# DeltaNet on one core: 64-row inverses applied twice with A's block between, side work after every third matmul, another order of the last two head blocks

## The chip, the cores and the metric

The kernel runs on one core of a Trainium2 chip. The metric is the device time of one execution in microseconds; lower is better. The core has a matrix engine (TensorE, PE in the rows, with its weight loads as PEld), a vector engine (VectorE, DVE), ScalarE (ACT), GpSimd (POOL) and DMA queues, of which SyncE (SP) and POOL issue most here.

## The reference

One layer of a streaming encoder over 16 meta rows plus 1024 prompt rows, and over 64 rows of a running stream. `xn = RMSNorm(h)` goes through one input projection of 2048 x 8208; 1024 channels feed a gated short convolution (mixer A) and 8 heads of 128 a gated DeltaNet (mixer B); an output projection of 2048 x 2048, a residual and a last RMSNorm follow. Mixer B works in chunks of 64 rows (cut, and written shorter):

```python
    kk = jnp.einsum('nbhid,nbhjd->nbhij', kc * bc[..., None], kc) * decay
    a_mat = jnp.where(strict, kk, 0.0) + eye
    t_mat = lax.linalg.triangular_solve(a_mat, eye, left_side=True, lower=True, unit_diagonal=True)
    u = t_mat @ (vc * bc[..., None])
    w = t_mat @ (kc * (bc * jnp.exp(gc))[..., None])
    qk = jnp.einsum('nbhid,nbhjd->nbhij', qc, kc) * decay

    def step(s, inp):
        v_new = u_i - w_i @ s
        o = (q_i * jnp.exp(g_i)[..., None]) @ s + qk_i @ v_new
        s = s * jnp.exp(g_last) + (k_i * jnp.exp(g_last - g_i)[..., None]).T @ v_new
        return s, o
```

The result of a chunk's `step` depends on the state `s` of the chunk before it; `t_mat` does not.

## The kernel before

The 1104 rows are the free dimension, in three pieces of 336, 384 and 384 columns. All weights and activations of the projections are split into a high and a low part, so that a product of two float32 numbers is three fast matmuls (high by high, low by high, high by low). A **job** is one tile of 128 output channels: 16 slices `k` of the contraction, three pieces, three matmuls, so 144 main matmuls into the PSUM tiles `pj`. There are 64 tiles: mixer A's block j has four jobs (AC, AX, AZ, AB), a head of mixer B has four (K, Q, V, Z). The string `order` sets in which order these blocks of four jobs run. After each job its PSUM tiles are read by VectorE, convolved and gated (the list `convs`), and written to DRAM scratch.

The DeltaNet of a head works in three steps p of three chunks of 128 rows each, 24 steps in all. Each is a **front** (`dn_front`) and later a **back** (`dn_back`). The front transposes q and k for their norms (PE `psq`, `psk`), builds the decays, multiplies k with k and q (PE `psm`), and gives three matrices A of 128 rows (`bm`) over DRAM to GpSimd, which inverts their 32-row diagonal blocks by elimination: DMA `e_in<-bm` on SP, then on POOL the DMA `eT<-e_in`, 60 small operations (`tm`, `eT`), the DMA `e_out<-eT` and the DMA `t<-e_out` back into the tile `t32` (`t` in the rows). The back waits for that tile. It adds the identity and transposes it in 32-row blocks on DVE (`t<-t,cst`, `ti<-t`), joins the blocks of 32 to 64 rows (`psx`, `psy` of 128 columns), then those of 64 to 128 rows (a second `psy`, `psx`, `psy`, each three matmuls of 64 x 64), and transposes v (`psv`). Then follow three chunks, one after the other: `psr` (k by the state) and r on DVE, `psu` (the inverse by r) and u on ACT, `psn` with the new state sn, and two matmuls into `po` for the output. After the third chunk the outputs are normalised on DVE (`on`) and transposed (`pot`).

PE takes its instructions in one order, with fronts and backs as **side work** between the main matmuls. A planner in the kernel sets that order while the program is written. It keeps estimated clocks `clk` of PE, DVE and ACT (`mm`, `tr` and the class `Timed` advance them). Front and back are generators: after `yield d` the next step is due at the largest of the three clocks plus d. `pump()` is called between main matmuls and writes out each step that is due by the PE clock; it also writes steps of `convs` while DVE's clock is less than 0.7 us ahead of PE's. A back starts when `el_done`, the planner's due time of the elimination, has passed: GpSimd is taken to be busy for `EL[1]` us from `EL[0]` us after the front's last step, or from the end of the elimination before. At most one finished front waits for its back, besides the one being written. On DVE the program order is kept; on PE and ACT the framework's scheduler may move instructions a little against the order in which they were written.

After the next-to-last job the fronts and backs left over are run to their end; then come the last job and the output projection, with `po` matmuls of 512 columns.

All vector operations are recorded at L61 (the helper), matmuls at L83, transposes on PE at L87.

Of the kernel before, what the change touches and what calls it, by code (L numbers as in the profile page):

```python
# [17 lines left out]
P = 128  # L18
# [48 lines left out]
def hymba_kernel(ctx: ExitStack, tc: tile.TileContext, hT, x_prompt, x_sample, w_in, w_ba, w_out, cst1, cst2, par,  # L67
# [348 lines left out]
    NFIRST = len(jobs)  # L416
    order = "b0 b1 b2 b3 a2 b4 a3 b5 a4 b6 a5 b7 a6 a7"
    for o in order.split():
# [8 lines left out]
    def project(js, first=lambda k: None, pool=pj):  # L427
# [5 lines left out]
        for kc in range(0, NK, 4):  # L433
            for kind, i, w, pieces in js:
                wh, wl = stream[0].get()
                first(kc)
                for k in range(kc, kc + 4):
                    for p in pieces:
                        a, n = 0 if p else SKIP[kind, w], PIECES[p][1]
                        o = ps[kind, i, w, p][:, a:n]  # L440
                        mm(o, wh[:, k - kc, :], xh[p][:, k, a:n], k == 0, False)
                        mm(o, wh[:, k - kc, :], xl[p][:, k, a:n], False, False)
                        mm(o, wl[:, k - kc, :], xh[p][:, k, a:n], False, k == NK - 1)
                    pump()
        flush_convs()
# [317 lines left out]
    def psd(name):  # L763
        return pd.tile([P, 4, P], F32, tag="pd", name=name)

    EL = (5.0, 50.0)
    t32 = [dn.tile([P, 3, P], F32, tag=f"t32_{i}", name=f"t32_{i}") for i in range(2)]
    for i in range(2):
        V.memset(t32[i], 0.0)
        Q.dma_start(whole(e_out[i]), t32[i])  # L770

    def dn_front(h, p):
# [58 lines left out]
        for c in range(3):  # L831
            pm = psd("psm")
            mm(pm[:, 0:2, :], kq[:, c, 0, :], kq[:, c, :, :], True, True)
            V.scalar_tensor_tensor(bm[:, c, :], pm[:, 0, :], cq[:, 9 + c:10 + c], bm[:, c, :], ALU.mult, ALU.mult)
            V.tensor_tensor(at[:, c, :], pm[:, 1, :], at[:, c, :], ALU.mult)
            yield 0.0
# [21 lines left out]
    def dn_back(h, p):  # L858
# [7 lines left out]
        V.transpose(ti.rearrange("p c t -> p (c t)"), tn.rearrange("p c t -> p (c t)"))  # L866
        b32 = tmp("b32", "b32", 1)
        V.tensor_tensor(b32, bm, cst[:, None, C_M32:C_M32 + P].to_broadcast([P, 3, P]), ALU.mult)
        yield 0.3
        px = psd("psx")  # L870
# [3 lines left out]
        S.copy(x, px[:, 0:3, :])  # L874
        yield 0.3
        py = psd("psy")
# [3 lines left out]
        V.tensor_tensor(tt, ti, py[:, 0:3, :], ALU.add)  # L880
        py2 = psd("psy2")
        for c in range(3):
            mm(py2[:64, c, 0:64], x[0:64, c, 0:64], tn[0:64, c, 0:64], True, True)
        t64 = b32[0:64, :, 64:128]
        V.tensor_tensor(t64, tn[0:64, :, 0:64], py2[0:64, 0:3, 0:64], ALU.add)
        yield 0.3
        px2 = psd("psx2")
        for c in range(3):
            mm(px2[0:64, c, 0:64], bm[64:128, c, 0:64], tt[64:128, c, 64:128], True, True)
        y64 = b32[0:64, :, 0:64]  # L890
        S.copy(y64, px2[0:64, 0:3, 0:64])
        yield 0.3
        py3 = psd("psy3")
        for c in range(3):
            mm(py3[0:64, c, 0:64], t64[:, c, :], y64[:, c, :], True, True)
        S.copy(tt[0:64, :, 64:128], py3[0:64, 0:3, 0:64])

# [12 lines left out]
        else:  # L910
            yield 0.3
        po = po_.tile([P, 4, P], F32, tag="po", name="po")
        for c in range(3):
# [8 lines left out]
            else:  # L922
                mm(pr[:, 0, :], kq[:, c, 0, :], s, True, True)
                V.scalar_tensor_tensor(r, pr[:, 0, :], cq[:, 6 + c:7 + c], vb[:, c, :], ALU.mult, ALU.add)
            yield 0.25
            pu = psd("psu")
# [19 lines left out]
            state[h] = sn  # L946
            yield 0.2
        if p == 2:
# [306 lines left out]
```

## Time and profile before

| | |
|---|---|
| three runs | 2256.23 us median, 2255.58 to 2258.77 |
| the profiled execution | 2254.53 us, of which its span from the first to the last instruction 2252.7 us |
| PE busy | 2200.5 us (98%) |
| DVE busy | 1346.3 us (60%) |
| POOL busy | 877.6 us (39%) |
| ACT busy | 603.0 us (27%) |
| mean granted TensorE clock | 0.997 |

A float32 matmul of the side work is one instruction in the program and two records in the trace, a main matmul is one in both. A matmul's end in the trace is modelled and lies beyond the start of the next, so the price of a matmul is read from starts, not from its duration.

### The profile page before, as it was taken

The numbers are of one execution on the slowest core, as the hardware profiler recorded it, in microseconds if no ns is written. First come the engines' busy times: TensorE is split into PE (matmuls) and PEld (weight loads), VectorE is DVE, ScalarE is ACT, GpSimd is POOL, SyncE is SP. The second block draws the span as 40 slices with busy tenths as digits, with TensorE's granted clock in tenths as the row PEclk, the third lists the DMA queues.
The fourth block names the chain that finished last, engine by engine and source line by source line (L and its number), as shares of the span: only waits on it lengthen the run. The fifth ranks groups of instructions, "written<-read, shape, count | busy, mean of one in ns | idle before, by whom it ended". The sixth has DMA issues, their size and how long they took to land.

```text
span 2252.7 us, 35780 instructions
## 1 busy us (share of the span) xinstructions
PE 2200.5 (98%) x12938; PEld 2065.4 (92%) x12938; DVE 1346.3 (60%) x3538; ACT 603.0 (27%) x1482; POOL 877.6 (39%) x1517
## 2 busy tenths in 40 slices
PE   8999999999999999999999999999999999999997
PEld 8999899999999999999999999999999987788886
DVE  6653475777675557565765576557664445474544
ACT  7232121222222122221222222122222125444341
POOL 0000038374666656455565666655564400000000
PEclk9999999999999999999999999999999999999999
DMA  7223132232222222322222222222322138664652
GB/s 261 77 88 94 39 92 80 81 94 81 90 74 88 66 64 85 89 67 78 91 87 64 75 79 89 63 73 78 94 70 75 50 126 270 208 198 147 224 169 84
DMA packets 162068, 231.13 MB, mean 103 GB/s; under 512 B 17756, under 2 KB 89636, under 8 KB 161764
## 3 DMA queue, kind: packets, MB, share of 16 engines
q1 hardware_dynamic: 156356, 217.30, 30.8%
q0 software_dynamic: 3072, 7.11, 1.6%
q10 hardware_dynamic: 2464, 4.46, 0.5%
q8 instruction: 101, 1.65, 0.3%
q14 instruction: 75, 0.61, 0.1%
HBM read 184.61 MB, written 44.17 MB: 102 GB/s over the span
## 4 chain that ended last, share of the span: by engine, by line
PE 87%; DVE 9%; DMA 2%; ACT 1%; issue 1%; SPq 0%; DVEq 0%; ACTq 0%
PE pj L83 61%; PE po L83 17%; DVE acc L61 3%; PE psy L83 2%; PE psx L83 1%; DMA yr<-yscr 1%; PE psm L83 1%; DVE wl L61 1%; PE psn L83 1%; PE pjb L83 1%; PE psu L83 1%; PE psr L83 1%; ACT jk L61 1%; DVE rot L61 1%; PE psv L87 1%
## 5 line engine op out<-in xcount | busy, mean ns | idle before, releaser
L83 PE MATMUL pj<-xh,wh 128*128 128x384 f32 x2048 | 692.9, 339 | 11.7 <-DVE raw L61 4.2
L83 PE MATMUL pj<-xl,wh 128*128 128x384 f32 x2048 | 690.6, 337 | 1.0 <-DVE xl L61 1.0
L83 PE MATMUL pj<-xh,wl 128*128 128x384 f32 x2048 | 688.5, 337 | 0.0
L61 DVE TENSOR_TENSOR wl<-wr,wh 128x512 fp32r<-128x512 f32 x464 | 337.3, 729 | 334.5 <-ACT wh L61 329.7
L83 PE MATMUL pj<-x,wh 128*128 128x320 f32 (+3 forms) x2048 | 522.3, 335 | 7.0 <-ACT x L61 7.0
L61 ACT CAST wh<-wr 128x512 fp32r<-128x512 f32 x464 | 285.9, 618 | 864.0 <-PE pj L83 666.6
L847 POOL TENSOR_TENSOR tm<-eT 12x30 f32<-12x30 f32 (+4 forms) x720 | 399.8, 555 | 122.9 <-DMA eT<-e_in 68.3
L849 POOL TENSOR_TENSOR eT<-eT,tm 12x30 f32<-12x30 f32 (+4 forms) x720 | 422.9, 587 | 56.4
L83 PEld LDWEIGHTS pj<-xh,wh 128*128 128x128 f32 x2048 | 385.3, 188 | 17.8 <-issue 5.8
L83 PEld LDWEIGHTS pj<-xl,wh 128*128 128x128 f32 x2048 | 385.0, 188 | 2.5 <-DVE xl L61 1.7
L83 PEld LDWEIGHTS pj<-xh,wl 128*128 128x128 f32 x2048 | 384.8, 188 | 0.0
L83 PEld LDWEIGHTS pj<-x,wh 128*128 128x128 f32 x2048 | 350.0, 191 | 16.5 <-ACT x L61 7.3
L83 PE MATMUL pj<-x,wl 128*128 128x320 f32 (+3 forms) x1024 | 320.8, 313 | 6.2 <-DVE wl L61 6.2
L842 POOL DMA_DIRECT2D eT<-e_in x24 | 17.4, 723 | 639.6 <-DMA e_in<-bm 326.6
L83 PE MATMUL po<-wh,yh 128*128 128x512 f32 x656 | 238.8, 396 | 3.1 <-DVE yh L61 2.8
L83 PE MATMUL po<-wl,yh 128*128 128x512 f32 x528 | 209.0, 397 | 1.9 <-DVE wl L61 1.9
L83 PEld LDWEIGHTS pj<-x,wl 128*128 128x128 f32 x1024 | 194.3, 190 | 7.8 <-DVE wl L61 7.8
L1113 POOL TENSOR_TENSOR hres<-hres,fw 128x512 f32<-128x512 f32 x1 | 1.7, 1732 | 469.4 <-ACT hres L61 469.4
L83 PEld LDWEIGHTS po<-wh,yh 128*128 128x128 f32 x656 | 123.1, 188 | 34.8 <-DVE yh L61 4.0
L61 DVE SCALAR_TENSOR_TENSOR acc<-raw,pk,acc 128x384 f32<-128x384 f32 (+1 forms) x216 | 147.3, 682 | 6.1
L83 PE MATMUL po<-wh,yl 128*128 128x512 f32 x336 | 132.8, 395 | 0.0
L83 PEld LDWEIGHTS po<-wl,yh 128*128 128x128 f32 x528 | 99.1, 188 | 27.1 <-DVE wl L61 3.4
(243 smaller groups left out, 2140.2 us busy)
## 6 DMA issues: line engine op xcount, KB each, us to landing
wr<-in_w_in SPq DMA_DIRECT2D x288, 256.0 KB, 3.1
wr<-in_w_out SPq DMA_DIRECT2D x176, 256.0 KB, 2.8
scr<-acc SPq DMA_DIRECT2D x48, 192.0 KB, 2.3
kq<-scr SPq DMA_DIRECT2D x48, 192.0 KB, 3.2
hres<-in_x_prompt SPq DMA_DIRECT2D x32, 256.0 KB, 5.2
yr<-yscr SPq DMA_DIRECT2D x32, 192.0 KB, 3.3
scr<-co SPq DMA_DIRECT2D x24, 192.0 KB, 1.9
gr<-gscr SPq DMA_DIRECT2D x24, 192.0 KB, 3.4
```

The costliest lines, as they stand in the source:

```text
L61: return fn(out, *a, **k)
L83: T.matmul(out, lhsT, rhs, start=start, stop=stop)
L87: T.transpose(out, in_, idn)
L842: G.dma_start(eT, blocks(e_in[i]))
L847: G.tensor_tensor(t, eT[:, j + 1:32, j:j + 1].to_broadcast([12, n, j]), eT[:, j:j + 1, 0:j].to_broadcast([12, n, j]), ALU.mult)
L849: G.tensor_tensor(eT[:, j + 1:32, 0:j], eT[:, j + 1:32, 0:j], t, ALU.add)
L1113: G.tensor_tensor(o, o, fw[:r, ns], ALU.mult)
```

## The change

Five edits. The second half of the inverse is no longer formed: per chunk, the block-diagonal inverse of 64-row blocks is multiplied with r, the result with A's lower left 64 x 64 block (kept transposed in `b64`), that is added to the lower half of r, and the inverse is applied again. `pump()` is called after every piece of a slice (three main matmuls) and not after every slice (nine). The distances `yield d` in the back grow from 0.2 to 0.3 us to 0.8 us. `EL[1]` falls from 50 to 43. The last head block runs before block 5 of mixer A.

```diff
-    order = "b0 b1 b2 b3 a2 b4 a3 b5 a4 b6 a5 b7 a6 a7"
+    order = "b0 b1 b2 b3 a2 b4 a3 b5 a4 b6 b7 a5 a6 a7"
...
                         mm(o, wl[:, k - kc, :], xh[p][:, k, a:n], False, k == NK - 1)
-                    pump()
+                        pump()
...
-    EL = (5.0, 50.0)
+    EL = (5.0, 43.0)
...
+    b64 = dn.tile([P, 3, P], F32, tag="b64", name="b64")
+    V.memset(b64, 0.0)
...
             V.scalar_tensor_tensor(bm[:, c, :], pm[:, 0, :], cq[:, 9 + c:10 + c], bm[:, c, :], ALU.mult, ALU.mult)
+            V.tensor_tensor(bm[0:64, c, 64:P], pm[0:64, 0, 64:P], at[0:64, c, 64:P], ALU.mult)
             V.tensor_tensor(at[:, c, :], pm[:, 1, :], at[:, c, :], ALU.mult)
...
-        b32 = tmp("b32", "b32", 1)
+        S.copy(b64[0:64, :, 64:P], bm[0:64, :, 64:P])
+        b32 = bm
         V.tensor_tensor(b32, bm, cst[:, None, C_M32:C_M32 + P].to_broadcast([P, 3, P]), ALU.mult)
-        yield 0.3
+        yield 0.8
...
         V.tensor_tensor(tt, ti, py[:, 0:3, :], ALU.add)
-        py2 = psd("psy2")
-        for c in range(3):
-            mm(py2[:64, c, 0:64], x[0:64, c, 0:64], tn[0:64, c, 0:64], True, True)
-        t64 = b32[0:64, :, 64:128]
-        V.tensor_tensor(t64, tn[0:64, :, 0:64], py2[0:64, 0:3, 0:64], ALU.add)
-        yield 0.3
-        px2 = psd("psx2")
-        for c in range(3):
-            mm(px2[0:64, c, 0:64], bm[64:128, c, 0:64], tt[64:128, c, 64:128], True, True)
-        y64 = b32[0:64, :, 0:64]
-        S.copy(y64, px2[0:64, 0:3, 0:64])
-        yield 0.3
-        py3 = psd("psy3")
-        for c in range(3):
-            mm(py3[0:64, c, 0:64], t64[:, c, :], y64[:, c, :], True, True)
-        S.copy(tt[0:64, :, 64:128], py3[0:64, 0:3, 0:64])
...
-            yield 0.25
+            yield 0.8
+            pu = psd("psu")
+            mm(pu[:, 0, :], tt[:, c, :], r, True, True)
+            u = dn.tile([P, P], F32, tag="u1", name="u1", bufs=1)
+            S.copy(u, pu[:, 0, :])
+            yield 1.05
+            pu = psd("psu")
+            mm(pu[:, 0, :], b64[:, c, :], u, True, True)
+            V.scalar_tensor_tensor(r[64:128], pu[64:128, 0, :], cq[64:128, 9 + c:10 + c], r[64:128], ALU.mult,
+                                   ALU.add)
+            yield 0.8
             pu = psd("psu")
             mm(pu[:, 0, :], tt[:, c, :], r, True, True)
...
             state[h] = sn
-            yield 0.2
+            yield 0.8
```

**The first place** is PE's order around one chunk in the middle of the program: before, from `psr` (k by the state) to `psu` (the inverse by r). `pj` are main matmuls, the size is that of the output.

```order
L83 MATMUL psr<-sn,kq 128x128
L83 MATMUL pj_11451<-x_241,wh 128x324 x2
L83 MATMUL pj_11451<-x_241,wl 128x324
L83 MATMUL pj_11452<-xh_244,wh 128x384
L83 MATMUL pj_11452<-xl_245,wh 128x384
L83 MATMUL pj_11452<-xh_244,wl 128x384
L83 MATMUL pj_11453<-xh_1310,wh 128x384
L83 MATMUL pj_11453<-xl_1311,wh 128x384
L83 MATMUL pj_11453<-xh_1310,wl 128x384
L83 MATMUL psu<-r,ti 128x128
```

In the change, `psu` stands there three times, the middle one with A's block `b`; what lies between the second and the third:

```order
L83 MATMUL psu<-u_11270,b_2875 128x128
L83 MATMUL pj_10999<-xh_244,wh 128x384
L83 MATMUL pj_10999<-xl_245,wh 128x384
L83 MATMUL pj_10999<-xh_244,wl 128x384
L83 MATMUL pj_11000<-xh_1310,wh 128x384
L83 MATMUL pj_11000<-xl_1311,wh 128x384
L83 MATMUL pj_11000<-xh_1310,wl 128x384
L83 MATMUL pj_10998<-x_241,wh 128x320 x2
L83 MATMUL pj_10998<-x_241,wl 128x320
L83 MATMUL psu<-r,ti 128x128
```

Nine main matmuls stand between two steps of the chain here, as before, but the chain has two steps more per chunk, and a step can now begin between two pieces of a slice (here after the first piece, `pj_10998`), where before it stood ahead of the first.

**The second place** is PE at the program's end: the last `pot` (transpose of the last back's output) of before, which stands 42 main matmuls into the last job; 102 main matmuls follow it up to the output projection.

```order
L83 MATMUL pj_19614<-x_241,wh 128x320 x2
L83 MATMUL pj_19615<-xh_244,wh 128x384
L83 MATMUL pj_19615<-xl_245,wh 128x384
L83 MATMUL pj_19616<-xh_1310,wh 128x384
L83 MATMUL pj_19616<-xl_1311,wh 128x384
L87 MATMUL pot<-cst,on 128x128 x3
L83 MATMUL pj_19614<-x_241,wl 128x320
L83 MATMUL pj_19615<-xh_244,wl 128x384
L83 MATMUL pj_19616<-xh_1310,wl 128x384
```

The scheduler has put five matmuls of the job ahead of `pot` and their three partners with the low weights behind it. In the change the same instruction stands in the third job from the end, with 423 main matmuls behind it:

```order
L83 MATMUL pj_19410<-xh_1310,wh 128x384
L83 MATMUL pj_19410<-xl_1311,wh 128x384
L83 MATMUL pj_19410<-xh_1310,wl 128x384
L87 MATMUL pot<-cst,on 128x128 x3
L83 MATMUL pj_19408<-x_241,wh 128x322 x2
L83 MATMUL pj_19408<-x_241,wl 128x322
```

The last back has moved by 321 main matmuls, more than two jobs, and nothing is left to run to its end after the next-to-last job.

**The third place** is DVE where a back begins, before: the third `psm` of the next front is read, then the back takes the inverted blocks `t`.

```order
L61 SCALAR_TENSOR_TENSOR bm<-psm,cq,bm 128x128
L61 TENSOR_TENSOR at<-psm,at 128x128
L61 TENSOR_TENSOR t_0_2888<-t_0_2888,cst 128x384
L61 STREAM_TRANSPOSE ti<-t_0_2888 128x384
L61 TENSOR_TENSOR b_18706<-bm,cst 128x384
```

The same in the change:

```order
L61 SCALAR_TENSOR_TENSOR bm<-psm,cq,bm 128x128
L61 TENSOR_TENSOR bm<-psm,at 64x64
L61 TENSOR_TENSOR at<-psm,at 128x128
L61 TENSOR_TENSOR wl<-wr,wh 128x512
L61 TENSOR_TENSOR kq<-kq,gr 128x3x128
L61 TENSOR_TENSOR t_0_2873<-t_0_2873,cst 128x384
L61 STREAM_TRANSPOSE ti<-t_0_2873 128x384
L61 TENSOR_TENSOR bm<-bm,cst 128x384
```

A small operation is added per chunk. From a front's third `psm` to the first `psx` of its own back PE's order holds 372 main matmuls on average before (351 to 400, the first two steps left out) and 316 in the change (288 to 357). From the last `po` of a back to its `pot` it holds 45 in 20 of 24 backs before, and in the change 39 to 42 in 16 of 24, and 20 to 27 in three.

## Rows read from the trace of the kernel before

**Rows 1.** The page: span, PE, and the chain that ended last, by engine.

```profile
span 2252.7 us, 35780 instructions
...
PE 2200.5 (98%) x12938; PEld 2065.4 (92%) x12938; DVE 1346.3 (60%) x3538; ACT 603.0 (27%) x1482; POOL 877.6 (39%) x1517
...
PE 87%; DVE 9%; DMA 2%; ACT 1%; issue 1%; SPq 0%; DVEq 0%; ACTq 0%
```

**Rows 2.** Groups by form, PE: count of records, busy us, mean ns.

```profile
L83 PE MATMUL psu<-r,ti 128*128 128x128 f32 x144 | 28.6, 280 | 2.0 <-DVE r L61 1.9
...
L83 PE MATMUL psx<-ti,bm 64*64 64x64 f32 x144 | 13.4, 226 | 0.0
```

**Rows 3.** Timeline of PE around one back: start us, duration us, instruction.

```profile
625.80 0.34 PE L83 MATMUL pj<-xh,wl 128*128 128x384 f32 x1
625.98 0.83 PE L83 MATMUL psy<-x,t 128*128 128x128 f32 x6
626.74 0.56 PE L83 MATMUL psy<-t,x 64*64 64x64 f32 x6
...
627.64 0.32 PE L83 MATMUL pj<-x,wl 128*128 128x336 f32 x1
...
628.66 0.33 PE L83 MATMUL pj<-xh,wl 128*128 128x384 f32 x1
...
629.15 0.32 PE L83 MATMUL pj<-x,wl 128*128 128x336 f32 x1
...
630.17 0.34 PE L83 MATMUL pj<-xh,wl 128*128 128x384 f32 x1
630.44 0.56 PE L83 MATMUL psx<-ti,bm 64*64 64x64 f32 x6
...
631.35 0.32 PE L83 MATMUL pj<-x,wl 128*128 128x336 f32 x1
...
636.57 0.34 PE L83 MATMUL pj<-xh,wl 128*128 128x384 f32 x1
636.75 0.38 PE L83 MATMUL psu<-r,ti 128*128 128x128 f32 x2
...
637.27 0.32 PE L83 MATMUL pj<-x,wl 128*128 128x336 f32 x1
```

**Rows 4.** Timeline of PE: the last back's transpose, and what follows.

```profile
1825.90 0.34 PE L83 MATMUL pj<-xl,wh 128*128 128x384 f32 x1
1826.95 0.55 PE L87 MATMUL pot<-cst,on 128*128 128x128 f32 x3 [0.70 <-DVE on L61]
1828.80 0.41 PE L83 MATMUL pj<-x,wl 128*128 128x320 f32 x1 [1.31 <-DVE wl L61]
```

**Rows 5.** Waits of PE: who waited for whom, us in total, times, longest.

```profile
PE pj L83 <- DVE raw L61: 4.2, 4, 1.9
...
PE psm L83 <- DVE kn L61: 2.5, 2, 2.1
PE psu L83 <- DVE r L61: 1.9, 4, 0.7
...
PE pot L87 <- DVE on L61: 1.0, 2, 0.7
```

**Rows 6.** Timeline of PE: a `psu` that waited.

```profile
642.24 0.34 PE L83 MATMUL pj<-xh,wl 128*128 128x384 f32 x1
642.92 0.49 PE L83 MATMUL psu<-r,ti 128*128 128x128 f32 x2 [0.34 <-DVE r L61]
...
643.55 0.32 PE L83 MATMUL pj<-x,wl 128*128 128x336 f32 x1
```

**Rows 7.** The tile `t`: count, durations, first and last start; then issue to landing.

```profile
L851 POOL DMA_DIRECT2D t<-e_out x24: 777/782/785, 360.5 to 1775.9; - x24
L61 DVE TENSOR_TENSOR t<-t,cst x24: 547/554/887, 373.3 to 1795.7; 128x384 f32<-128x384 f32 x24
...
DMA to landing us min/median/max: 2.8/3.0/4.9
```

More of the change, by code (lines that the diff above doesn't have):

```diff
@@ L880, in dn_back @@
         V.tensor_tensor(tt, ti, py[:, 0:3, :], ALU.add)
-        py2 = psd("psy2")
-        for c in range(3):
-            mm(py2[:64, c, 0:64], x[0:64, c, 0:64], tn[0:64, c, 0:64], True, True)
-        t64 = b32[0:64, :, 64:128]
-        V.tensor_tensor(t64, tn[0:64, :, 0:64], py2[0:64, 0:3, 0:64], ALU.add)
-        yield 0.3
-        px2 = psd("psx2")
-        for c in range(3):
-            mm(px2[0:64, c, 0:64], bm[64:128, c, 0:64], tt[64:128, c, 64:128], True, True)
-        y64 = b32[0:64, :, 0:64]
-        S.copy(y64, px2[0:64, 0:3, 0:64])
-        yield 0.3
-        py3 = psd("psy3")
-        for c in range(3):
-            mm(py3[0:64, c, 0:64], t64[:, c, :], y64[:, c, :], True, True)
-        S.copy(tt[0:64, :, 64:128], py3[0:64, 0:3, 0:64])
         pv = psd("psv")
@@ L910, in dn_back @@
         else:
-            yield 0.3
+            yield 0.8
         po = po_.tile([P, 4, P], F32, tag="po", name="po")
@@ L924, in dn_back @@
                 V.scalar_tensor_tensor(r, pr[:, 0, :], cq[:, 6 + c:7 + c], vb[:, c, :], ALU.mult, ALU.add)
-            yield 0.25
+            yield 0.8
[8 more added lines that the diff above has]
+                                   ALU.add)
+            yield 0.8
             pu = psd("psu")
@@ L946, in dn_back @@
             state[h] = sn
-            yield 0.2
+            yield 0.8
         if p == 2:
```

## The prediction

> **What bounds the kernel.** I read the page first: PE is busy for 98% of the span of 2252.7 us, and the chain that ended last lies on PE for 87% of it [rows 1]. The span is therefore a long row of matmuls plus the moments at which PE's next one is not ready, and a change is worth what it takes out of that row or adds to it. Busy time cannot price a matmul here, because records overlap. So the second view is the timeline of PE, read from start to start. Without side work, one matmul of 384 columns and two of 336 take 629.15 - 628.66 = 0.49 us, and the nine of a slice 630.17 - 628.66 = 1.51 us, 0.168 us each [rows 3]. What a piece of side work costs is the same stretch with it inside, less 0.49 us. Third come the waits of PE, small throughout [rows 5], and fourth the elimination on GpSimd, whose result a back needs [rows 7].
>
> **The matmuls removed and added.** A back loses three groups of three matmuls of 64 x 64. One group alone costs 631.35 - 630.17 - 0.49 = 0.69 us [rows 3]. Another, behind the `psy` group of 128 columns, gives 627.64 - 625.80 - 0.49 = 1.35 us for both, 0.67 us each if they cost alike. So a 64-row matmul costs about 0.225 us. An inserted `psu` of 128 rows costs 637.27 - 636.57 - 0.49 = 0.21 us, and the 128-column group says 0.67 / 3 = 0.22 us [rows 3]. The small matmuls are, in PE's time, no cheaper than the large ones. Per back 9 x 0.225 = 2.03 us go and 6 x 0.22 = 1.32 us come (three chunks, two `psu` more in each; the 72 `psu` of before are the 144 records of [rows 2]). The difference of 0.71 us over 24 backs is **-17 us**; with 0.21 against 0.23 us it is -19, with 0.22 against 0.215 us -15.
>
> The Trainium skill, TensorE: Matmul & The Clock Gate, section Back-to-back issue gap, has matmuls spaced by their columns over 2.4 GHz plus a fixed 2.5 ns, so that with the four passes of a float32 product 64 columns cost about half of 128. By that estimate, 0.12 against 0.22 us, the 216 small matmuls give back 25 us and the 144 new ones cost 32, and the change would lose 7 us. The trace agrees with it for 128 columns and not for 64, where it shows 0.69 us for three.
>
> **The end.** Before, the last back's `pot` waits for DVE, and behind it the matmuls that the scheduler held back wait for `wl`, which stands behind that back's work on DVE: from 1825.90 to 1828.80 us PE starts one main matmul and three transposes, some 0.5 us of work [rows 4]. In the change the last back ends in the third job from the end, under main matmuls: **-2.4 us**. The order of the blocks does nothing else to PE: the jobs are the same.
>
> **New waits in the chain.** Each chunk has two dependent steps more, `psu` to u on ACT to `psu` with A's block to r on DVE to `psu`: 144 new places at which PE can find its operand late. Before, 4 of 72 `psu` found r late, 1.9 us in all [rows 5]; the idle time is counted from the end of the record ahead, which lies beyond the point where PE could have gone on, so I price such a wait by starts: 643.55 - 642.24 - 0.49 - 0.21 = 0.61 us where the row says 0.34 [rows 6]. By 0.61 / 0.34 the 72 cost 3.4 us, and 144 alike would cost 6.8 us. The least distance rises from 0.25 to 0.8 us, which should take the shortest cases away, but a step placed in the first piece after a chunk of weights now stands behind that chunk's `wl` on DVE. The bounds are 0 and 22 us (0.15 us at each); I take **+4 us**, between nothing and the rate of before.
>
> **Steps that come nearer.** `pot` keeps its 3.2 us, but `pump` rounds up to 0.5 us now instead of 1.5, and the order shows 39 to 42 main matmuls ahead of most and 20 to 27 ahead of three, for 45 before. Five fewer are 0.8 us. Before, `pot` waited 1.0 us in all, and that at two places [rows 5]; a third of the 24 would now be short by some 0.3 us and the three by 0.5 to 1: **+3 us**, bounds 0 and 10. The second `psy` group is treated likewise, with a scheduler that puts some of them four main matmuls behind `psx`: **+1 us**. Against that, PSUM of a finished job is read sooner when the convolutions have not been left to the job's end; the largest such wait is 4.2 us in 4 [rows 5], and I take **-2 us** for all of its kind, bounds -8 and +4.
>
> **The elimination.** This is what the lower `EL[1]` brings near. The first back's DMA is issued at 360.5 us and lands 3.0 us later, and DVE takes the tile at 373.3: a margin of 9.8 us. For the last it is 1795.7 - 1775.9 - 3.0 = 16.8 us [rows 7]. Over all 24, each with its own landing, the mean is 13.9 us, the least 8.5. In the change 372 - 316 = 56 main matmuls fewer stand between front and back, 56 x 0.168 = 9.4 us, and the longer first distance of the back takes another 0.5 us: the mean margin falls to 4 us, with a scatter of some 4 us either way. Most are still on time; a few in 24 are late by 1 to 3 us, and then DVE stands at `t<-t,cst` with the weights' `wl` queued behind it, and PE at `psx`. **+4 us**, bounds 0 and 15.
>
> Where I cost an edit at nothing: DVE gains two small operations per chunk (r's lower half and a 64 x 64 product) and loses one per back; it is idle for 40% of the span [rows 1], and only its lateness counts, which is priced above. ACT's copies lie in 73% idle time. The output projection and the prologue keep their work.
>
> **The sum.** -17 - 2.4 + 4 + 3 + 1 - 2 + 4 = -9.4 us against the profiled execution's 2254.5 us, 2245.1 there. The profiled execution lies 1.7 us below the median of 2256.2; against the median the sum gives **2247 us**, 0.4% less. What this kernel's measurement can tell from no change is about 0.2%, 4.5 us.
>
> **Rivals.**
>
> *The waits stay as they are.* The larger least distance does its work and the elimination is on time: only -17, -2.4 and -3 for the waits at PSUM and r are left, 2234 us. For it: waits of PE on side work are a few microseconds in all [rows 5]. Against it: the margins become smaller in three of the places.
>
> *The elimination is late (slower).* If GpSimd's chain does not fit the planner's 43 us, the mean margin is not 4 but below zero. Each further microsecond by which 24 backs are late costs up to 24 us, since `psx` stands in PE's order. It decides at a mean lateness of about 0.6 us (13.4 / 24), and at 1 us the time is 2247 - 4 + 24 = 2267 us. For it: the least margin of before, 8.5 us, is already less than the 9.9 us taken away. Against it: that is one of 24, and the mean is well above.
>
> *The chain's steps wait (slower).* If each of the 144 new places costs 0.15 us, the term is 22 instead of 4 and the time 2265 us. It decides at 0.09 us per place (13.4 / 144). Before it was 3.4 / 72 = 0.05.
>
> *Small matmuls are cheap (slower).* If the price follows the records, the three small groups give back 3 x 13.4 = 40 us and twice 28.6 = 57 us come [rows 2]: with the other terms 2256 + 17 + 8 = 2281 us. The starts speak against it. By the estimate from TensorE: Matmul & The Clock Gate in the Trainium skill it would be 2256 + 7 + 8 = 2271 us.
>
> *Nothing much.* The new waits eat the whole gain: 2256 us.
>
> **How the numbers follow.** The likeliest is the sum, 0.50, with a range of its own of 2240 to 2254 us. Waits as they are: 0.20. Elimination late: 0.10. Chain waits: 0.10. Cheap small matmuls: 0.03. Nothing much: 0.07. Faster by over 0.2% (below 2251.7) holds the second case and about four fifths of the first, with a little of the last: 0.62. Slower (above 2260.7) holds the three slow ones but for their mild ends: 0.18. Within: 0.20. The range leaves out the far part of the slow cases and the lowest part of the fast one: 2232 to 2262 us.
>
> **What would show it.** In the profile after: 288 more records of `psu` and 432 fewer of 64 x 64; an inserted `psu` still at 0.21 us from start to start; no wait of `pot` in the last job; waits of PE on u and r of 4 to 8 us, on `on` of 2 to 4 us; the gap on DVE before `t<-t,cst` waiting for the DMA `t<-e_out`, new, in a few of 24. Wrong would make me: DVE waiting for that DMA in most backs, PE idle before `psx`, or waits before `psu` above 10 us.

## The result, and the profile after

The changed kernel takes **2289.2 us** (median of 4 runs, 2288.2 to 2291.3) against 2257.5 us beside it: a ratio of **1.0143, 95% interval 1.0131 to 1.0156**. It is slower by 1.4%, where 0.4% less was forecast, and lies outside the range. One disturbed execution, of 9048 us in the run with the new inverse alone, is left out below. The page of its profiled execution:

```profile
span 2288.2 us, 35657 instructions
...
PE 2203.6 (96%) x12794; PEld 2076.7 (91%) x12794; DVE 1389.6 (61%) x3659; ACT 611.6 (27%) x1530; POOL 868.9 (38%) x1517
...
PE 34%; DVE 6%; POOL 2%; DMA 2%; issue 1%; ACT 1%; DVEq 0%; SPq 0%; POOLq 0%; ACTq 0%
```

Beside [rows 1], the span is 35.5 us longer (2288.2 - 2252.7) while PE's busy time grew by 3: by the page, the loss is idle time of PE. The chain that ended last runs on PE for 34% instead of 87%; it now leaves PE often. The groups by form show that the work is the one forecast, 288 more `psu` and no matmul of 64 x 64 [rows 2]:

```profile
L83 PE MATMUL psu<-r,ti 128*128 128x128 f32 x288 | 57.7, 282 | 15.2 <-DVE r L61 15.2
...
L83 PE MATMUL psu<-u,b 128*128 128x128 f32 x144 | 28.6, 280 | 0.3 <-ACT u L61 0.3
...
L83 PE MATMUL psx<-ti,bm 128*128 128x128 f32 x144 | 20.7, 280 | 6.4 <-DVE bm L61 6.4
```

PE's waits (in total, times, longest) answer to [rows 5]:

```profile
PE psu L83 <- DVE r L61: 15.2, 16, 2.1
PE pot L87 <- DVE on L61: 11.2, 9, 2.7
PE pj L83 <- DVE raw L61: 9.6, 4, 3.9
...
PE psx L83 <- DVE bm L61: 6.4, 9, 1.1
PE psr L83 <- DVE sn L61: 4.8, 7, 2.0
...
PE psm L83 <- DVE kn L61: 1.4, 3, 0.6
```

`psu` waits eight times as long as before, `pot` eleven times; `psx` and `psr`, now at 6.4 and 4.8 us, waited 0.3 us each before. Of the 15.2 us at `psu`, 11.0 fall on the third of a chunk, which reads the corrected r (11 of 72 wait), and 4.2 on the first, the step that was there before (2.0 then, by the same count). The middle one, which reads u, waits 0.3. One such wait on PE's timeline, and what it leaves behind (start, duration, instruction):

```profile
1130.72 0.31 PE L83 MATMUL pj<-x,wl 128*128 128x336 f32 x1
1130.87 0.38 PE L83 MATMUL psu<-u,b 128*128 128x128 f32 x2
...
1131.26 0.33 PE L83 MATMUL pj<-xl,wh 128*128 128x384 f32 x1
...
1132.45 0.32 PE L83 MATMUL pj<-x,wl 128*128 128x336 f32 x1
...
1132.78 0.34 PE L83 MATMUL pj<-xl,wh 128*128 128x384 f32 x1
1132.96 0.34 PE L83 MATMUL pj<-xh,wl 128*128 128x384 f32 x1
1135.44 0.49 PE L83 MATMUL psu<-r,ti 128*128 128x128 f32 x2 [2.15 <-DVE r L61]
1135.68 0.51 PE L83 MATMUL pj<-xh,wh 128*128 128x384 f32 x1
1136.00 0.52 PE L83 MATMUL pj<-xl,wh 128*128 128x384 f32 x1
```

The inserted `psu` costs what was forecast: (1131.26 - 1130.72) - (1132.78 - 1132.45) = 0.21 us. The next one, twelve main matmuls later, finds r late, and behind it main matmuls start 0.32 us apart instead of 0.17. The windows view shows why (per stretch: its length, then the busy time of PE, PEld, DVE, ACT and POOL, the granted clock, the DMA share and GB/s):

```profile
1128.00:1132.00 4.00, 4.00 (x27) 4.00 (x26) 3.34 (x7) 1.26 (x3) 3.56 (x6) 1.00 0.21 62
1132.00:1136.00 4.00, 1.85 (x12) 1.53 (x11) 3.90 (x7) 0.03 (x1) 3.69 (x5) 0.98 0.14 50
1136.00:1139.40 3.40, 3.40 (x13) 3.40 (x13) 2.74 (x5) 0.75 (x2) 3.09 (x5) 0.52 0.26 76
1139.40:1143.00 3.60, 2.79 (x20) 2.50 (x19) 3.23 (x5) 0.86 (x3) 3.29 (x5) 1.00 0.15 55
```

After the gap TensorE ran at its lower level, 1.2 GHz, from 1136.0 to 1139.4 us, which cost another 1.5 us. There are seven such stretches of 3.4 us ahead of the output projection, for two in the kernel before, and no term of the prediction held them. DVE's timeline shows why r was late:

```profile
1131.20 1.10 DVE L61 SCALAR_TENSOR_TENSOR co<-raw,acc 128x64 f32<-128x64 f32 x3 [0.55 <-ACT raw L61]
1132.26 0.10 DVE L61 MEMSET co<- 128x48 f32 x1
1132.33 0.73 DVE L61 TENSOR_SCALAR acc<-raw,pk 128x384 f32<-128x384 f32 x1
1133.10 0.85 DVE L61 SCALAR_TENSOR_TENSOR acc<-raw,pk,acc 128x384 f32<-128x384 f32 x1
1133.87 1.13 DVE L61 TENSOR_TENSOR wl<-wr,wh 128x512 fp32r<-128x512 f32 x1
1135.03 0.36 DVE L61 SCALAR_TENSOR_TENSOR r<-psu,cq,r 64x128 f32<-64x128 f32 x1
```

Convolution steps and a `wl` stand ahead of it, the last two at 0.85 and 1.13 us, where the next `acc` of the same shape takes 0.62.

To see the whole I added up PE's starts up to the first matmul of the output projection: each distance less the price of what lies in it (0.168 us or so per main matmul by its columns, 0.22 per 128-row matmul, 0.23 per 64-row one). What is left goes to the side step that had the largest gap, to a main matmul, or, where the distance touches a stretch at 1.2 GHz, whole to that stretch, so that the last column holds some waits too. Worked out from the traces, in us (the runs with "cut" come below):

```
                          first    side  waits of  waits of    of these      excess in
                          out proj work  pj        side steps  psu psr pot psx  1.2 GHz stretches
before                    1846.7   235.3  28.6      23.1        4   4   3   1    3.1
changed                   1883.6   219.1  26.4      65.0       20  12  11   9   16.2
before, cut               1827.1   235.3  14.7      17.5        1   3   3   1    3.2
changed, cut              1820.4   219.1   9.3      26.8        2   5   4   5    8.0
third alone               1889.2   235.3  21.7      44.5        6  11  14   4   33.2
third alone, cut          1820.0   235.3   9.5      16.0        1   5   2   1    4.4
changed, roots in PSUM    1867.6   219.1  23.0      56.7       21  17   1   8   12.3
```

So the change took 16.2 us of work from PE, as forecast, and brought 41.9 us of waits of side steps and 13.1 us more in the stretches at 1.2 GHz. Of these 13.1 the clock itself can hold 8.5 at most: at half the clock, seven stretches of 3.4 us lose 11.9 us and two lose 3.4. The rest are waits that end beside a stretch, above all a `psu` of 2.5 us (the one shown) and a `pot` of 3.0.

### The profile page after: what moved, and what is told of

Read it like the earlier page. It is cut to its first block, busy times and chain, and to the rows that moved or that the text cites. A ratio compares the mean times of both kernels' runs of the same rounds, so it can differ in the third digit from the quotient of the medians.

```text
span 2288.2 us, 35657 instructions
## 1 busy us (share of the span) xinstructions
PE 2203.6 (96%) x12794; PEld 2076.7 (91%) x12794; DVE 1389.6 (61%) x3659; ACT 611.6 (27%) x1530; POOL 868.9 (38%) x1517
## 5 line engine op out<-in xcount | busy, mean ns | idle before, releaser
L83 PE MATMUL pj<-xh,wh 128*128 128x384 f32 x2048 | 722.9, 354 | 13.3 <-DVE raw L61 9.6
L83 PE MATMUL pj<-x,wh 128*128 128x320 f32 (+3 forms) x2048 | 496.4, 322 | 6.5 <-ACT x L61 6.5
L83 PEld LDWEIGHTS pj<-x,wh 128*128 128x128 f32 x2048 | 361.6, 190 | 9.0 <-ACT x L61 6.5
```

The lines of the kernel that those rows point to most:

```text
L83: T.matmul(out, lhsT, rhs, start=start, stop=stop)
```

## The experiments

Ratios are to the kernel before, run beside each on the same chip; times are medians. "Third" is short for `pump` at every third main matmul, the due time is `EL[1]`.

**The change taken apart.** Four theories were on record for these: C, that `pump` at every third matmul puts convolution steps ahead of the chain's on DVE; E, that the lower due time moves fronts and backs onto each other; N, that 144 new steps cost whatever the grid; and D, that the longer back runs into the end of the main matmuls.

*`pump` once per slice again:*

```diff
-                        pump()
+                    pump()
```

> The changed kernel with side work again at every ninth main matmul, all other edits kept. Theory C (side work at every third matmul lets the planner write out convolution steps sooner, so that the chain's small vector steps stand behind them on DVE): most of the 48 us of new waits go, about 2255 us or below, waits of psu on r under 5 us for 15.2. Theory E (the lower due time of the elimination brings fronts and backs on top of each other): little changes, 2280 us or more. Theory N (the 144 new dependent steps cost it whatever the grid): 2280 us or more, and psu still waits 15 us.

2277.4 us, 1.0089 (1.0074 to 1.0104): 12 us of the 32 come back, though 13 us of side work now stand bare, with no main matmul between, behind the next-to-last job. Waits of `psu` on r fall from 15.2 to 4.1 us. The time lies between theory C's number and the others'.

*The changed kernel with `EL = (5.0, 50.0)`:*

> The changed kernel with EL[1] at 50 again, all else kept. Theory E: the waits before psx, psr and pot go down, 2265 us or less, and DVE no longer waits for the inverted blocks (10.3 us in 4 places). Theory C and theory N: within 6 us of the changed kernel, 2283 to 2290 us, for DVE's wait for the blocks is 10 us of an engine with slack.

2307.2 us, 1.0218 (1.0202 to 1.0234), slower still: 25 us of the last back stand bare. Theory E, which had the lower due time as the loss, falls here; with 50 the longer back runs bare at the end.

*Convolutions issued once per slice, side work at every third matmul:*

```diff
-    def pump():
+    def pump(conv=True):
...
-        while convs and clk["dve"] - clk["pe"] < 0.7:
+        while conv and convs and clk["dve"] - clk["pe"] < 0.7:
...
-                        pump()
+                        pump(p == pieces[-1])
```

> The changed kernel in which fronts and backs may still be written at every third main matmul, but convolution steps only at every ninth. Theory C: as good as side work per slice, about 2255 to 2262 us. If it is the finer grid of the chain itself (less rounding up, so less slack for pot and psr) and not the convolutions: 2280 us or more, psu waits fall a little, pot waits stay at 11 us. Theory E and theory N: 2280 us or more.

2274.2 us, 1.0075 (1.0058 to 1.0092): 15 us come back, half of them at `psu`. Theory C is borne out by half: 17 us of the 32 stay.

*The kernel before with third alone:*

> The kernel before with one edit alone, side work at every third main matmul (its distances of 0.2 to 0.3 us kept). Theory C: slower than before by 15 to 40 us, 2272 to 2297 us, for the same convolutions stand ahead of r and sn, and the distances are shorter. Theory E and theory N: within 6 us of before, 2251 to 2263 us.

**2295.9 us**, 1.0173 (1.0154 to 1.0192): one moved line costs the kernel before 39 us, more than the whole change. Of its side steps `pot` waits longest, then `psr`.

*The kernel before with the same, convolutions per slice:*

> The kernel before with fronts and backs allowed at every third main matmul and convolution steps per slice as before. Theory C (convolutions ahead on DVE): most of the 39 us that side work at every third cost this kernel go, 2257 to 2270 us. If it is the finer grid of the chain with short distances: 2285 us or more.

2294.1 us, 1.0171 (1.0148 to 1.0195): theory C does not hold for the kernel before; its loss comes with the places of fronts and backs.

*The kernel before with the new inverse alone:*

> The kernel before with the new inverse alone (distances of the old size, side work per slice, EL[1] 50, old order of blocks). In PE's order 36 side matmuls then stand in one place behind the next-to-last job, with no main matmul between them. Theory D (the longer back lengthens the loop of front, elimination and back, which is close to the time that the jobs give it, so the last backs run bare at the end): about 2257 - 17 + 20 to 25 us for that stretch + 4, 2260 to 2270 us, and the stretch is seen at the end. Theory N (the 144 new steps wait wherever they stand): 2275 us or more, with psu waiting over 10 us on r.

2310.6 us, 1.0233 (1.0202 to 1.0264). The last back stands bare for 58 us, where theory D had 20 to 25; apart from that, side steps wait 30 us, `psu` on r 5.9 of them, less than theory N asks for. Without the lower due time the new inverse cannot be judged.

*The kernel before with a due time of 47 and the new order of blocks:*

```diff
-    order = "b0 b1 b2 b3 a2 b4 a3 b5 a4 b6 a5 b7 a6 a7"
+    order = "b0 b1 b2 b3 a2 b4 a3 b5 a4 b6 b7 a5 a6 a7"
...
-    EL = (5.0, 50.0)
+    EL = (5.0, 47.0)
```

> The kernel before with EL[1] at 47 and the new order of the last blocks, nothing else. The last pot then has 378 main matmuls behind it, for 102. Theory D: the wait of the last pot and of the matmuls behind it goes, 2 to 5 us faster than before, 2252 to 2255 us. Theory E (a shorter due time brings fronts and backs onto each other): 2262 us or more.

2269.6 us, 1.0061 (1.0042 to 1.008). The end is no longer late, and yet 13 us are lost: ahead of the output projection side steps wait 11 us more, `pot` first, and 10 us more (13.2 for 3.1) go in the stretches at 1.2 GHz, six for two, waits beside them included.

*The changed kernel with `pump` per slice and the short distances (0.2 and 0.3 us) of before:*

> The changed kernel with side work per slice and the distances of the old size (0.2 to 0.3 us); new inverse, EL[1] 43 and the new order stay. Nothing is left bare at the end (144 main matmuls behind the last pot). Theory D: the 2277 us of side work per slice alone less its bare stretch of 13 us, 2260 to 2268 us. Theory N: 2275 us or more, since shorter distances only add waits.

2270.1 us, 1.0067 (1.0047 to 1.0088), the best recombination of the parts, and still no gain.

**Where the waits come from.** Two theories: U, that the planner's DVE clock is too fast and the coarse grid hid it; and P, that DVE's operations take longer while GpSimd eliminates.

*The changed kernel with the elimination cut to one step ("cut"):*

```diff
-        for j in range(1, 31):
+        for j in range(1, 2):
```

> The changed kernel with GpSimd's elimination cut to its first step (j = 1 only; the inverses of the 32-row blocks and so the output are left incomplete). TensorE's order is that of the changed kernel. Theory P (the small DVE operations of the chain ahead of pot take 0.45 to 0.5 us instead of 0.16 while GpSimd's elimination runs, and so on comes 7.3 instead of 5.0 us behind the last po): the pot waits of 10.7 us fall to below 3, those of psr and psu by a third or more, half-clock stretches with them; 2260 to 2272 us. Theory U (DVE's operations simply take longer than the planner's clock says, and the finer grid of the chain took away the slack that hid it): GpSimd matters little, psu and psr waits stay at 32 us; 2280 to 2289 us, a few us below the changed kernel for the places where DVE waited for the elimination (10 us on DVE).

**2227.4 us**, 0.9858 (0.9843 to 0.9873): 62 us less than the changed kernel with the same order on PE, and 33 below theory P's range. The third `psu` of a chunk waits 0.2 us in all, for 11.0. DVE's groups by form in the changed kernel (busy us, mean ns):

```profile
L61 DVE TENSOR_TENSOR wl<-wr,wh 128x512 fp32r<-128x512 f32 x464 | 337.9, 730 | 363.3 <-ACT wh L61 361.1
L61 DVE SCALAR_TENSOR_TENSOR acc<-raw,pk,acc 128x384 f32<-128x384 f32 x144 | 98.7, 686 | 4.4
...
L61 DVE SCALAR_TENSOR_TENSOR r<-psr,cq,vb 128x128 f32<-128x128 f32 x64 | 22.2, 347 | 44.2 <-PE psr L83 44.2
...
L61 DVE SCALAR_TENSOR_TENSOR rot<-rot,so 128x3 f32<-128x3 f32 x72 | 17.4, 242 | 2.5
```

and with the cut:

```profile
L61 DVE TENSOR_TENSOR wl<-wr,wh 128x512 fp32r<-128x512 f32 x464 | 318.9, 689 | 374.3 <-ACT wh L61 371.0 <-DMA wr<-in_w_out 1.1
L61 DVE SCALAR_TENSOR_TENSOR acc<-raw,pk,acc 128x384 f32<-128x384 f32 x144 | 88.9, 618 | 4.4
...
L61 DVE SCALAR_TENSOR_TENSOR r<-psr,cq,vb 128x128 f32<-128x128 f32 x64 | 22.3, 349 | 49.3 <-PE psr L83 49.2
...
L61 DVE SCALAR_TENSOR_TENSOR rot<-rot,so 128x3 f32<-128x3 f32 x72 | 11.6, 162 | 2.5
```

The operations with two operands in SBUF shrink, those that read PSUM (`r<-psr`) do not. The changed kernel's own trace says the same without a second run: the 39 of the 72 `rot<-rot,so` that meet no elimination operation of GpSimd take 0.162 us (0.165 at most), the 33 that do 0.337 on the average. DVE's busy time falls from 1389.6 to 1279.2 us with the same 3659 instructions. `rot<-rot,so`, of three elements, takes 160/161/507 ns (least, median, longest) in the changed kernel and 160/161/165 with the cut. Up to nine of them in a row lead from the last `po` to `on`: with the cut `on` ends 5.0 us after it in 17 of 24 backs and 6.6 at most, without it up to 8.3.

The Trainium skill, SBUF — State Buffer, section SBUF: two separate sides, says that DVE and GpSimd share a pair of SBUF ports under an exclusive lock, that a DVE operation in a two-port performance mode takes it, as does one with two inputs from SBUF against a GpSimd operation that reads SBUF, and that the loser waits for the whole instruction. The rows agree, in that operations with two inputs from SBUF grow and one of three elements can take 0.3 us longer; that the lock is what holds them is taken from that section, the runs show the stretching.

*The changed kernel with the planner's DVE clock set to the trace (0.17 us + 0.00135 per element), least distances of the back 0.1 us (one more edit of this run empties `convs` where the first weights of the output projection are fetched):*

```diff
-    V = Timed(nc.vector, clk, "dve", 0.09, 0.00104)
+    V = Timed(nc.vector, clk, "dve", 0.17, 0.00135)
```

> The changed kernel with the planner's DVE clock set to what the trace shows (0.17 us + 0.00135 us per element, for 0.09 + 0.00104) and the least distances of the back cut to 0.1 us, since the clock now carries the time. Theory U: the planner places psu, psr and psx behind the true end of their operands; side waits fall from 65 us to 25 or 30 and half-clock stretches to below 8; 2240 to 2258 us. Theory P, or the convolutions' turn on DVE alone: the clock has no part for GpSimd, pot waits stay near 10 us and psu waits are halved at most; 2270 to 2280 us.

2328.1 us, 1.0315 (1.0292 to 1.0337), the slowest of all. PE's waits:

```profile
PE pj L83 <- DVE raw L61: 16.9, 11, 5.4
PE pot L87 <- DVE on L61: 15.1, 4, 4.9
PE pj L83 <- DVE xt L61: 11.9, 7, 4.0
PE pj L83 <- DVE zr L61: 8.9, 5, 4.3
...
PE psu L83 <- DVE r L61: 0.7, 2, 0.5
```

The waits that theory U is about do go, with GpSimd at work: `psu` on r waits 0.7 us for 15.2, and `psr` and `psx` are gone from the list. But main matmuls now wait for the convolution steps that read their PSUM (`raw`, `zr`), and the stretches at 1.2 GHz ahead of the output projection grow from seven to thirteen. So the mechanism of theory U holds at these steps, and its time does not: the chain's waits were exchanged for the convolutions'.

*Third alone, with 0.5 us added to every least distance and a due time of 46:*

> The kernel before with side work at every third matmul, as in the run that had this alone, and 0.5 us added to every least distance of front and back (half of the 1.0 us by which the grid of places became finer), with a due time of 46 for 50 so that the last backs are not left bare. Theory U: what the finer grid took away is given back; side waits fall from 44.5 us to about those of before (23), half-clock stretches from 33 to below 10 us; 2250 to 2265 us. Theory C (the convolutions stand ahead of the chain on DVE because they are issued at every third matmul): added distance helps little, 2280 to 2296 us. Theory E (a lower due time moves fronts and backs onto each other): 10 to 14 us above before, 2267 to 2272 us.

2286.4 us, 1.0123 (1.0105 to 1.014): 10 of the 39 us come back, within theory C's range. By the rows, main matmuls wait 2.9 us on `wl` for 13.8, and the stretches at 1.2 GHz ahead of the output projection fall from 34 us in all to 20; side steps wait about as long (`pot` 12.7 us for 13.3, `psr` 8.6 for 10.9, `psu` 3.4 for 4.8, `psx` 7.9 for 2.8). The order shows that the added distance does not bring the old places back: from `psr` to `psu` six main matmuls stand in 33 of 72 cases and nine in 25, for nine in 60 before; from `po` to the next `psr` six in 39 of 48, for nine in 44.

*The changed kernel with 5.5 us for 3.2 ahead of `pot`:*

> The changed kernel with 5.5 us for 3.2 as pot's least distance. Theory P and U alike: pot's waits of 10.7 us and the half-clock stretches behind them (3 of the 8, some 1.7 us each, 5 us) go, 14 to 16 us in all: 2273 to 2277 us. If the longer back only moves its waits to psu, psr and psm of the next blocks: 2283 to 2292 us.

2289.6 us, 1.0137 (1.0122 to 1.0152): `pot`'s waits go (10.7 to 3.7 us), and `psr`'s rise from 12.3 to 20.9. Here the wait was moved and not saved; why `psr` waits longer was not looked into.

**What GpSimd costs each kernel.** Three further runs ask whether before carries the same cost.

*The kernel before with the cut:*

> The kernel before with the same cut of GpSimd's elimination (its first step alone; the inverses of the 32-row blocks and so the output are incomplete). Theory P, that the change exposed the chain to GpSimd and the kernel before was covered by its wider distances: before gains 10 to 20 us, 2238 to 2248, and the changed kernel with the cut (2227) leads it by about the 17 us that the work of TensorE promises, with 2 for the end. Theory G, that GpSimd costs both kernels alike and the change's loss is its finer grid: before gains as much as the changed kernel did, 50 to 60 us, 2197 to 2207, and still leads it by 20 to 30.

2235.0 us, 0.9903 (0.9884 to 0.9922): before gains 22 us where the changed kernel gained 62. Its engines, for [rows 1]:

```profile
PE 2192.5 (98%) x12938; PEld 2065.8 (93%) x12938; DVE 1236.0 (55%) x3538; ACT 603.3 (27%) x1482; POOL 71.3 (3%) x125
```

Between the two with the cut, the changed one leads by 7.7 us (2227.4 / 2235.0 = 0.997; 10 us by the two ratios), where theory P had some 17 and 2 more for the end. By the table it still waits 9.3 us longer at side steps, and 4.8 us more go in the stretches at 1.2 GHz.

*The changed kernel with the whole elimination, whose result no back waits for (the tile is read before the loop):*

```diff
+        G.dma_start(t32[i], whole(e_out[i]))
         tm = dn.tile([12, 240], F32, tag="tm", name="tm", bufs=1)
...
-        G.dma_start(t32[i], whole(e_out[i]))
```

> The changed kernel with the whole elimination on GpSimd, but the back reads the tile as the elimination of two blocks before left it, so that it waits for no result of its own (the output isn't the reference's). GpSimd's work is kept. If DVE's operations being slower under GpSimd is the cause: 2275 to 2290, with pot still waiting some 10 us and psu 15 to 20. If the late result of the elimination is the cause: near the 2227 of the cut, 2225 to 2240, with the waits of psr, psu and psx at the cut kernel's 12 us in all.

2290.2 us, 1.0143 (1.0122 to 1.0164), like the changed kernel. PE's waits:

```profile
PE psu L83 <- DVE r L61: 16.1, 15, 2.4
PE pot L87 <- DVE on L61: 11.7, 8, 3.0
...
PE psx L83 <- DVE bm L61: 6.1, 7, 1.5
```

That the result comes late costs nothing that these runs can tell (some 5 us either way); GpSimd at work is what costs.

*Third alone with the cut:*

> The kernel before with side work at every third matmul, and GpSimd's elimination cut to its first step (output incomplete, as above). Theory P: without GpSimd the distances are enough on the finer grid too, and it stays within 5 us of the kernel before with the same cut, 2235 to 2253 by that theory's number for it. Theory G: the finer grid costs its 39 us here too, 2236 to 2246 by that theory's 2197 to 2207 for the kernel before.

**2228.9 us**, 0.9875 (0.9858 to 0.9892): with GpSimd quiet the finer grid costs nothing, and may be worth 6 us; with GpSimd at work it costs 39. PE's waits with third alone:

```profile
PE pot L87 <- DVE on L61: 13.3, 11, 2.9
PE psr L83 <- DVE sn L61: 10.9, 8, 3.0
...
PE psu L83 <- DVE r L61: 4.8, 6, 2.1
```

and with the cut:

```profile
PE pot L87 <- DVE on L61: 3.5, 3, 2.7
...
PE psr L83 <- DVE sn L61: 0.5, 1, 0.5
```

**Taking the operands away.** The last runs put the iterates of both inverse square roots, the operations of 3 and 6 elements, into a free quarter of a PSUM tile, so that each reads one operand from PSUM and one from SBUF:

```diff
+    def rsqrt_in(ps, v, n):
+        y = ps[:, 3, 0:n]
...
+        for _ in range(3):
+            V.tensor_tensor(t, y, v, ALU.mult)
+            V.scalar_tensor_tensor(t, t, -0.5, y, ALU.mult, ALU.mult)
+            V.scalar_tensor_tensor(y, t, 1.5, y, ALU.add, ALU.mult)
...
-        ro = rsqrt_of(dn, ss, 3, "ro")
-        V.tensor_tensor(ro, ro, cq[:, 0:3], ALU.mult)
+        ro = dn.tile([P, 3], F32, tag="roy", name="roy")
+        V.tensor_tensor(ro, rsqrt_in(po, ss, 3), cq[:, 0:3], ALU.mult)
```

*In the changed kernel:*

> The changed kernel, with y of both inverse square roots in the unused quarter of a PSUM tile; same operations and count, one more small copy in each front. If operations with one operand in PSUM are not slowed by GpSimd (as r<-psr, sn<-psn and on<-po are not in the traces): the small operations take one length with and without GpSimd, on comes 5 to 6 us behind the last po in every back instead of 5.0 to 8.3, and pot's waits of 10.7 us fall to below 4, with some of the half-clock stretches: 2270 to 2278 us. If what slows them is a place in the queue and not the operand's memory: they still take 0.3 us on the average under GpSimd and the time stays at 2286 to 2293.

2273.7 us, 1.0077 (1.006 to 1.0094): 15.5 us less than without. The operations, under GpSimd's elimination, in the groups by form:

```profile
L61 DVE SCALAR_TENSOR_TENSOR po<-rt,po 128x3 f32<-128x3 f32 x72 | 12.0, 166 | 2.5
...
L61 DVE TENSOR_TENSOR rt<-po,so 128x3 f32<-128x3 f32 x72 | 11.5, 160 | 2.4
...
L61 DVE SCALAR_TENSOR_TENSOR rt<-rt,po 128x3 f32<-128x3 f32 x72 | 11.4, 158 | 2.5
```

They take 158 to 166 ns on the average where `rot<-rot,so` took 242. `on` ends 5.0 to 6.8 us after the last `po` in all backs but one, `pot`'s waits fall from 10.7 to 1.4 us; `psu` keeps its 20; the convolutions and `wl` ahead of r still read two operands from SBUF, which is the likely reason and was not tested. PE's order moves a little too (from `psr` to `psu` nine main matmuls in 38 of 72 cases, for 45), so not all of the 15.5 us need be the operations'.

*In the variant with convolutions per slice:*

> The same in the variant with the convolutions issued once per slice (2274 us without it, with pot's waits at 10.3 us and psm's at 7.4): 2256 to 2266 us if the small operations are the carrier, 2272 to 2278 if not.

2257.4 us, 0.9999 (0.9988 to 1.001), from 2274.2.

*In the variant with `pump` per slice and short distances:*

> The same in the variant with side work once per slice and the short distances of before (2270 us without it; psm waits 11.1 us for what follows the front's inverse square root, pot only 1.7): 2256 to 2266 us if the small operations are the carrier, 2268 to 2274 if not. The kernel before, at 2257, is likely not beaten by more than the measurement can tell.

2258.8 us, 1.001 (0.9999 to 1.0022), from 2270.1. The first is the best version with the new inverse; it equals the kernel before and does not beat it. The kernel before with its iterates in PSUM was not run.

## Why the prediction was wrong

- **The matmuls, -17 us**: -16.2 by the starts. A group of three was priced rightly, and for whole groups the rival in which small ones are cheap falls. The reason was read wrongly: inside a group of 64 x 64 the records start 0.058 us apart and a matmul has two of them, 0.117 us each, half of a 128-row one (0.11 per record, 0.22); [rows 3] has it too, six records in 0.56 us for 0.83. The price per group, 0.69 us, is 0.35 for the three and 0.34 at the two ends, where the shape changes: the first small record starts 0.27 us after the main matmul ahead (0.17 where 128 rows follow), and the next main matmul 0.15 us after the last small one (0.03 behind 128 rows). That this equals three large matmuls is luck of the number three. The prediction's estimate of 0.12 us for one holds inside a group; its "not for 64" reads the group's ends into the matmul.
- **The end, -2.4 us**: the last `pot` at 1812.26 us waits for nothing. Right, though its worth was not measured by itself; the order alone was not run.
- **`psu`, +4 us (0 to 22)**: +16.0 by starts (some 18 with the wait beside a stretch), within its bounds of 0 to 22 but four times the term. "144 alike" was wrong: the 72 new steps on u wait 0.3 us in all, the 72 on the corrected r 11.0, which is the 0.15 us each of the slow rival. The step behind the term failed: that the least distance of 0.8 us "should take the shortest cases away". A least distance is rounded up to the next place, and the places moved from 1.5 to 0.5 us apart. From `psr` to `psu` there were nine main matmuls in 60 of 72 cases before, and nine in 45 of 72 in the changed kernel, with twelve in eight; from the second `psu` to the third there are nine in 50 of 72. The typical step is no wider, and with GpSimd quiet the same order is wide enough. From `po` to the next `psr` there are six, for nine before.
- **`pot`, +3 us (0 to 10)**: +7.5, and some 3 more beside a stretch, about the upper bound. The places were read rightly (39 to 42 main matmuls for 45), but the time of `on` was not looked at: in the kernel before it already scatters from 5.0 to 9.5 us behind the last `po`, where 45 main matmuls are 7.6 us; with the cut 20 of its 24 are at 5.0. A step that varies that much can't be priced by its total wait.
- **`psr` (+8.5 us)** had no term. **`psx` (+8.5)** had one only as the result of a late elimination, and its rows wait as long where no result is waited for (6.1 for 6.4 us). `psy`'s +1 did not come.
- **PSUM's readers, -2 us**: -2.2 for waits of main matmuls, the right number by luck. The row it was read from, `pj` on `raw`, rose from 4.2 to 9.6 us; others fell.
- **The elimination, +4 us**: late as described, in 4 backs, and DVE waits for it:

```profile
L856 POOL DMA_DIRECT2D t<-e_out x24: 775/780/787, 358.0 to 1767.6; - x24
L61 DVE TENSOR_TENSOR t<-t,cst x24: 546/552/801, 361.8 to 1770.6; 128x384 f32<-128x384 f32 x24
...
  DMA t<-e_out: 10.3, 4
```

  The first margin is 361.8 - 358.0 = 3.8 us from issue to use, for 12.8 in [rows 7]. But without that wait the time stays (2290.2 us): its price is nothing that can be measured.
- **The lower clock**: no term; 13.1 us more in the stretches at 1.2 GHz, at most 8.5 of them the clock's own. A gap of PE was priced at its length; some are followed by such a stretch.

The sum that failed is thus that of the waits: 10 us forecast at side steps and at PSUM, and 39.7 measured (41.9 - 2.2), with 13.1 in the stretches at 1.2 GHz on top, waits in part. "DVE is idle for 40% of the span" was no cover, since what counts is when DVE's operation ends.

What the runs show of the cause: GpSimd at work makes DVE later than the planner's clock says, and the finer grid no longer covers it. Its elimination adds the same 110 us to DVE's busy time in the kernel before (1346.3 against 1236.0 with the cut), in the changed one and with third alone (1348.8 against 1238.0). On the grid of whole slices 22 us of it reach the end; on the grid of every third matmul 67, and in the change 62. Why 0.5 us more on each distance gave back only 10 of 39 us stays open; one reason is that a distance of 0.3 rounds to 1.5 us on the coarse grid and one of 0.8 to 1.0 on the fine one, as the six main matmuls for nine in that run's order show; a run with the old places on the fine grid was not made.

## What to carry over

Before moving the places of a dependent chain closer, look at the scatter of each step's ready time against its margin, and at what makes it scatter: here the same DVE operation takes 0.16 or up to 0.5 us, by whether GpSimd is at work. A coarse grid can be hidden slack: an edit that issues work "as soon as allowed" spends it. Where small DVE operations stand on the path beside GpSimd, keep one operand in PSUM: that gave 11 to 17 us here.

## What the runs showed of the hardware

- GpSimd's operations on 12 partitions stretch DVE's operations with two SBUF operands (three elements: from 0.16 to as much as 0.5 us; `wl`: from 0.69 to 0.85 on the average where they overlap, in the changed kernel), and do not stretch those with one operand in PSUM (`r<-psr` 0.347 against 0.349 us).
- A one-input operation from SBUF is stretched as well: `rot<-so` takes 168/170/505 ns in the changed kernel and 169/170/171 with the cut.
- In the changed kernel a wait of PE of 2.15 us was followed by 3.4 us at a granted clock of 0.52, so that it cost 2.3 us and 1.5 more.
- In the kernel before, a float32 matmul of 64 x 64 starts 0.117 us behind another of its kind, one of 128 x 128 0.22 us; a group of three small ones among matmuls of 128 rows costs 0.69 us, 0.34 of it at its two ends.
